# A second FFN with six seven-product blocks in place of five, and a last norm whose weight is multiplied in with the factor

## The chip, the cores and the metric

One core of a Trainium2 chip runs the whole layer. The metric is the device time of one execution in microseconds. The kernel before takes 2642.25 us (median of three runs, 2641.42 to 2644.68).

The engines appear under these names: PE is TensorE's matrix unit (PEld its weight loads), DVE is VectorE, ACT is ScalarE, POOL is GpSimd, SP is SyncE, which here only issues DMAs. Each engine runs its own queue in order.

## What is computed

The layer is a diffusion backbone block: a half-step SwiGLU FFN, a mixer (attention heads beside mLSTM heads), a second half-step SwiGLU FFN, and a final RMSNorm. The change lies in the second FFN and the final norm, which work on the 256 latent tokens alone. With `D` = 2048 and `D_FF` = 5632:

```python
def rms_norm(x, g):
    y = xf * lax.rsqrt(jnp.mean(xf * xf, axis=-1, keepdims=True) + RMS_EPS)
    return (y * g.astype(jnp.float32)).astype(x.dtype)

def adaln(x, g, mod, i):
    return rms_norm(x, g) * (1 + mod[:, i + 1, None, :]) + mod[:, i, None, :]

def half_step_ffn(x, mod, i, g, w_up, w_down):
    h = adaln(x, g, mod, i)
    a, b = jnp.split(h @ w_up, 2, axis=-1)
    return x + 0.5 * mod[:, i + 2, None, :] * ((jax.nn.silu(a) * b) @ w_down)
...
        xl = half_step_ffn(xl, mod_l, 6, g_norm[l, 2], w_ffn2_up[l], w_ffn2_down[l])
...
    return rms_norm(xl, g_final)
```

Everything is float32.

## The kernel before

**Products.** A float32 product is made of three matmuls in a faster format (`mm3`, L143 on): each operand is split into a high part and a low remainder, and high x high, high x low and low x high are added up in PSUM. Activations are split once. Each weight tile of 128x2048 is loaded from memory into `raw` (three buffers) and split by `split` in two halves of 128x1024: ScalarE writes `hi` (L123), VectorE writes `lo = raw - hi` (L124). `hi` and `lo` have four buffers each, so at most four half tiles are ready ahead of PE.

**Blocks.** The 5632 columns of the FFN are 11 blocks of 512 (`FB` = 4 tiles of 128), numbered 0 to 10; `LAST` is 10. Block 0 is made before the loop. For each block there is an up projection (both halves, `a` and `b`) and a down projection. `down(n)` has four units, one for each column block `cb` of the output: it loads one tile of `w_dn`, makes 12 matmuls for each of the two groups of 128 tokens, and adds the result to `acc2` in SBUF.

**Two kinds of up projection.** `up(n)` is the plain one, eight units: 2 halves x 4 weight tiles, 24 matmuls each, 192 in all. `quad(n)` makes the same block with seven products for eight: the normed activations are seen as 2x2 quarters (128 tokens x 1024 inputs), the weights as 2x2 quarters (1024 inputs x half `a` or `b`), and seven products of sums of quarters replace eight of plain quarters. The sums of activations (`n1`, `s4`, `s2`, `s3`) are made once by `token_forms`. Each product is two steps (`q` = 0 and 1, one weight tile of 128x2048 each) of 12 matmuls, so a quad has 14 steps and 168 matmuls, collected in two PSUM banks `X` and `Y`.

**Sums of weights in a quad.** The products need the weight quarters B11; B11+B12; B11+B12+B22; and all four, in this order, in two SBUF tiles `chain_[q]`; and B22 and then B12+B22 in two tiles `ra[q]`. `chain_[q]` is loaded plainly through SP, and then each further quarter is added by an accumulating DMA which POOL issues (`accum`, L696), as soon as the tile has been split for the product before. `ra[q]` is loaded with B22 through SP (`loaded`) and receives B12 by an accumulating DMA. `again` loads the first quarter of the next quad into `chain_[q]` after the last product's split. The list `order` in `quad` names for every product its activations, its weight tile, its PSUM bank, what is to follow the split (`then`) and what is done with the bank (`use`).

**Order.** `units()` yields the up and down units of the blocks made plainly and of all down projections; after each unit `u` the loop at the end of the function takes steps of the quads, until `n_side` reaches `(u + 1) * PACE2`. The results of a block are turned by PE (`turned`, four transposes for a block and a group of 128 tokens) into the layout that the down projection reads (`hids`, two buffers); `turned` waits until block n - 2 has been summed up, and `done` notes which results have been turned. A scheduler then orders the instructions of each engine by priority, where nothing pins them; `tc.keep_in_program_order` pins one.

**Beside it.** `beside["load"]` is an iterator which `load_split` advances once for every plain unit: it carries the 32 items of the modulation rows 8 (`mod_late`, a VectorE multiply-and-sum of 128x1024 for each, L203), and at their end `mod_rows_out` (L355): a transpose, a copy by VectorE, and a DMA of the row to memory. `before_final` then loads that row into all partitions as `late["g8"]`, and the norm's weight as `late["gf"]`, into the places of `chain_`. The last down blocks need `g8` (`half_gated`, L980).

**The end.** Block 9's down projection adds the gate and, by an accumulating DMA, the residual to `acc2`. `last2` makes block 10's down projection and the final norm, for each group of 128 tokens: for each column block, gate (L982), add, square and sum on ScalarE (`sumsq`), multiply by `gf` (L2183). After the fourth sum: a reduction on VectorE, `rsqrt_mean` on POOL (two instructions: a multiply-add, and a power of -1/2), then the factor times the column blocks, shared between ScalarE and VectorE, and the output's DMAs.

Of the kernel before, what the change touches and what calls it, by code (L numbers as in the profile page):

```python
# [9 lines left out]
F32 = mybir.dt.float32  # L10
# [9 lines left out]
P = 128  # L20
# [13 lines left out]
PACE = (4, 2), (12, 13), (19, 19), (26, 28), (33, 37), (37, 44), (42, 51), (48, 54), (52, 61), (55, 70), (58, 76), (59, 85), (63, 96)  # L34
PACE += (70, 102), (72, 109), (75, 118), (76, 130), (77, 144), (80, 152), (83, 163), (85, 166), (86, 174), (96, 181)

PACE2 = 70 / 73

BLOCKS2 = tuple((k, k + 4) for k in range(0, 16, 4))

# [14 lines left out]
def tile_layer(ctx: ExitStack, tc: tile.TileContext, I: dict, out: bass.AP):  # L55
# [641 lines left out]
    with pool(name="f1u", bufs=1) as f1u:  # L697
# [16 lines left out]
        def part(n, ab, c):  # L714
            return I["w_up1b"][n - 1, ab, c]
# [1119 lines left out]
    with f2x:  # L1835
# [54 lines left out]


        LAST = NF // FB - 1
        QUADS = range(1, LAST, 2)

        def part(n, ab, c):
            return I["w_up2b"][n - 1, ab, c]
# [85 lines left out]
        def quad(n):  # L1982
# [38 lines left out]
            def chained(ab, c):  # L2021
                return lambda q: accum(chain_[q], part(n, ab, c + q))

            def again(q):
                if n + 2 in QUADS:
                    nc.sync.dma_start(chain_[q], part(n + 2, 0, q))

            def loaded(q):
                ra[q] = ra_tile()
# [3 lines left out]
            def plain(q):  # L2033
# [5 lines left out]
            order = (  # L2039
                (a11, held, "X", True, chained(1, 0), p1),  # L2040
                (a12, plain, "Y", True, None, c11),
                (n1, held, "Y", True, chained(1, 2), kept),
                (s4, loaded, "Y", False, lambda q: accum(ra[q], part(n, 1, q)), p35),
                (s2, held, "X", False, chained(0, 2), c12),
                (s3, lambda q: ra[q], "X", False, None, c22),
                (a22, held, "Y", True, again, c21),
# [49 lines left out]
        def down(n):  # L2096

            assert (n, 1) in done or not n
            for cb in range(NCB):
                wt = load_split(I["w_dn2"][n, cb])  # L2100
                for t in range(2):
                    c = slice(cb * CB, (cb + 1) * CB)
                    b = block(n, wt, t)
                    a = acc2[:, t, c]
                    if n == 0:
                        nc.scalar.activation(a, b, AF.Copy)
                    else:
                        nc.vector.tensor_tensor(a, a, b, op=ALU.add)
                    if n == LAST - 1:
                        half_gated(a, a, late["g8"][:, c])  # L2110
                        accum(a, x2d[t * P : (t + 1) * P, c])
                if cb == NCB - 1:
                    summed.add(n)
                yield

        def units():
            yield from up(2)
            yield from down(0)
            for n in (4, 6, 8):
                yield from up(n)  # L2120
                yield from down(n - 3)
                yield from down(n - 2)
            yield from down(7)
            yield from up(10)
            yield from down(8)

        def before_final():
            drain(beside["load"])
# [6 lines left out]
        def quads():  # L2135
            for n in QUADS:
                yield from quad(n)

        forms = token_forms()
        side, n_side, n_quads = quads(), 0, 14 * len(QUADS)  # L2140
        for u, _ in enumerate(units()):
            steps(forms)
            turned()
            while n_side < n_quads and n_side < (u + 1) * PACE2:
                next(side)
                n_side += 1
                turned()
# [7 lines left out]
        def last2():  # L2155

            parts = []
            for cb in range(NCB):
                if cb >= 2:
                    parts.append(load_split(I["w_dn2"][LAST, cb]))  # L2160
                    continue
                raw = raw_tile()
                nc.sync.dma_start(raw, I["w_dn2"][LAST, cb])
                hi = f3.tile([P, 2048], F32R, tag=f"f{2 * cb}", name=f"hi{cb}")
                lo = f3.tile([P, 2048], F32R, tag=f"f{2 * cb + 1}", name=f"lo{cb}")
                nc.scalar.activation(hi, raw, AF.Copy)
                nc.vector.tensor_tensor(lo, raw, hi.bitcast(F32), op=ALU.subtract)
                parts.append(lambda w, hi=hi, lo=lo: (hi[:, w], lo[:, w]))
            for t in range(2):
                ss = sm.tile([P, 4], F32, tag="ss4", name="ss4", bufs=4)  # L2170
                for cb in range(NCB):
                    c = slice(cb * CB, (cb + 1) * CB)
                    b = block(LAST, parts[cb], t)
                    a = acc2[:, t, c]
                    y = sab_tile()
                    half_gated(y, b, late["g8"][:, c])
                    nc.vector.tensor_tensor(a, a, y, op=ALU.add)
                    sumsq(ss[:, cb : cb + 1], a)
                    if cb == NCB - 1:
                        s1 = sm.tile([P, 1], F32, tag="s1", name="s1")  # L2180
                        nc.vector.tensor_reduce(s1, ss, axis=AX.X, op=ALU.add)
                        r = rsqrt_mean(s1, D)
                    nc.vector.tensor_tensor(a, a, late["gf"][:, c], op=ALU.mult)  # L2183
                for cb in range(NCB):
                    c = slice(cb * CB, (cb + 1) * CB)
                    a = acc2[:, t, c]
                    if t == 0 or cb % 2:
                        nc.scalar.activation(a, a, AF.Copy, scale=r)
                    else:
                        nc.vector.tensor_scalar(a, a, r, None, op0=ALU.mult)  # L2190
                    nc.sync.dma_start(out[t * P : (t + 1) * P, c], a)

        last2()

# [95 lines left out]
```

## Time and profile before

| what | us |
|---|---|
| median of three runs | 2642.25 |
| the profiled execution | 2649.92 |
| its span (first to last instruction) | 2648.2 |
| PE busy in the span | 2598.3 (98%) |
| VectorE busy in the span | 2123.5 (80%) |
| ScalarE busy in the span | 1365.9 (52%) |
| mean granted TensorE clock | 0.994 |

How to read the rows of the profile below. A row of the view by stretch gives the stretch in us, its length, the busy time and number of instructions of PE, PEld, DVE, ACT and POOL, the mean granted clock, the mean busy share of the 16 DMA engines and GB/s. A row of waits gives who waited for whom, the total in us, how often, and the longest. A row of the timeline gives the start in us, the duration, engine, line, operation and shapes; in brackets stands the idle time before it and what ended it. A row of the chain that ended last gives start, duration and instruction. A row of a group of instructions gives their number, busy time, mean ns of one, and the idle time of the engine just before them with what ended it. A row of DMA issues gives the number, the size of one and the median us from issue to landing; "DMA to landing" gives the shortest, median and longest of one line.

### The profile page before, as it was taken

To read this page: it belongs to the slowest core of one execution; us is meant where nothing else is said; L and a number is where in the kernel's file an instruction comes from. 1 tells how busy PE (TensorE), PEld (TensorE's weight loads), DVE (VectorE), ACT (ScalarE), POOL (GpSimd) and SP (SyncE) were. 2 spreads that over 40 slices of the span, in tenths; PEclk is the share of its full clock that TensorE was granted. 3 is DMA by queue.
4 is the path that set the end of the run, shared out by engine and by line. 5 is a ranking of instruction groups with operands and counts; after the bars stand their busy time and mean duration, and the time that the engine had idled before them with its cause. 6 is when DMAs were issued, how large, how long until landed. Compare 5 with 4: busy or idle time off the path is not lost. (4 is left out here: it accounts for less than half of the span.)

```text
span 2648.2 us, 33739 instructions
## 1 busy us (share of the span) xinstructions
PE 2598.3 (98%) x12718; PEld 2154.5 (81%) x12718; DVE 2123.5 (80%) x2854; ACT 1365.9 (52%) x1741; POOL 221.9 (8%) x271
## 2 busy tenths in 40 slices
PE   7999999999999999999999999999999999999998
PEld 4688887888788878888879989877898888888886
DVE  7697878878888788888887878788788777777867
ACT  4354444554444555444455438455476655555554
POOL 1000001000001000000111000111000000000001
PEclk8999999999999999999999999999999999999999
DMA  9879999999999989889986855666679998989975
GB/s 371 331 222 266 266 279 262 256 276 281 256 273 260 284 232 244 212 218 226 226 249 248 310 199 195 243 210 215 217 253 288 303 294 283 286 286 279 272 232 169
DMA packets 127219, 679.97 MB, mean 257 GB/s; under 512 B 14152, under 2 KB 16712, under 8 KB 65232
## 3 DMA queue, kind: packets, MB, share of 16 engines
q1 hardware_dynamic: 99696, 500.59, 50.9%
q0 software_dynamic: 27360, 177.22, 34.2%
q8 instruction: 100, 1.64, 0.2%
q14 instruction: 63, 0.52, 0.1%
HBM read 659.87 MB, written 17.89 MB: 256 GB/s over the span
## 5 line engine op out<-in xcount | busy, mean ns | idle before, releaser
L123 ACT ACTIVATE hi<-raw 128x1024 fp32r<-128x1024 f32 (+2 forms) x538 | 558.1, 1042 | 600.5 <-PE mm L147 454.0
L124 DVE TENSOR_TENSOR lo<-raw,hi 128x1024 fp32r<-128x1024 f32 (+1 forms) x524 | 630.6, 1210 | 254.0 <-ACT hi L123 229.6
L123 ACT ACTIVATE hi<-chain 128x1024 fp32r<-128x1024 f32 x320 | 337.8, 1059 | 259.0 <-PE mm L147 128.5
L124 DVE TENSOR_TENSOR lo<-chain,hi 128x1024 fp32r<-128x1024 f32 x320 | 387.1, 1221 | 99.3 <-ACT hi L123 96.8
L145 PE MATMUL mm<-hi,hhi 128*128 128x512 f32 (+3 forms) x1024 | 394.1, 386 | 7.0 <-DVE c L799 7.0
L147 PE MATMUL mm<-hi,hlo 128*128 128x512 f32 (+3 forms) x1024 | 388.4, 379 | 0.0
L146 PE MATMUL mm<-lo,hhi 128*128 128x512 f32 (+3 forms) x1024 | 388.0, 379 | 0.2
L203 DVE SCALAR_TENSOR_TENSOR junk<-sraw,cBh 128x1024 fp8e5<-128x1024 f32 x192 | 234.2, 1220 | 23.7 <-DMA sraw<-in_w_mt 21.4
L145 PEld LDWEIGHTS mm<-hi,hhi 128*128 128x128 f32 x1024 | 192.8, 189 | 39.6 <-ACT hi L123 4.5
L147 PEld LDWEIGHTS mm<-hi,hlo 128*128 128x128 f32 x1024 | 193.1, 189 | 33.9
L146 PEld LDWEIGHTS mm<-lo,hhi 128*128 128x128 f32 x1024 | 193.3, 189 | 31.8 <-DVE lo L124 0.6
L147 PE MATMUL mm<-hi,hid2l 128*128 128x512 f32 x352 | 137.4, 390 | 0.0
L145 PE MATMUL mm<-hi,hid2h 128*128 128x512 f32 x352 | 137.2, 390 | 0.0
L146 PE MATMUL mm<-lo,hid2h 128*128 128x512 f32 x352 | 137.1, 390 | 0.0
L145 PE MATMUL mm<-hi,h2hi 128*128 128x512 f32 x320 | 124.7, 391 | 0.6 <-DVE sab L1874 0.6
L146 PE MATMUL mm<-lo,h2hi 128*128 128x512 f32 x320 | 124.8, 390 | 0.1
L147 PE MATMUL mm<-hi,h2lo 128*128 128x512 f32 x320 | 124.6, 389 | 0.0
L696 POOL DMA_DIRECT2D chain<-in_w_up1b x60 | 53.1, 884 | 743.5 <-DVE lo L124 582.8
L145 PE MATMUL mm<-hhi,hi 128*128 128x512 f32 (+1 forms) x288 | 101.2, 351 | 0.0
L147 PE MATMUL mm<-hhi,lo 128*128 128x512 f32 (+1 forms) x288 | 99.0, 344 | 0.0
L146 PE MATMUL mm<-hlo,hi 128*128 128x512 f32 (+1 forms) x288 | 98.7, 343 | 0.0
L203 DVE SCALAR_TENSOR_TENSOR sr<-sr,cBl 128x1024 f32<-128x1024 f32 x65 | 78.9, 1225 | 8.7 <-DMA sr<-in_w_mt 8.6
(492 smaller groups left out, 5477.1 us busy)
## 6 DMA issues: line engine op xcount, KB each, us to landing
raw<-in_w_dn SPq DMA_DIRECT2D x70, 1024.0 KB, 7.4
sraw<-in_w_mt SPq DMA_DIRECT2D x128, 512.0 KB, 7.7
chain<-in_w_up1b POOLq DMA_DIRECT2D x60, 1024.0 KB, 10.7
raw<-in_w_up2b SPq DMA_DIRECT2D x50, 1024.0 KB, 7.0
raw<-in_w_up1b SPq DMA_DIRECT2D x40, 1024.0 KB, 8.2
mraw<-in_w_m SPq DMA_DIRECT2D x32, 1024.0 KB, 7.2
sr<-in_w_mt SPq DMA_DIRECT2D x62, 512.0 KB, 5.3
chain<-in_w_dn POOLq DMA_DIRECT2D x30, 1024.0 KB, 8.4
```

Of the source, the lines that this page charges most:

```text
L123: scalar[0].activation(hi, src, AF.Copy)
L124: vector[0].tensor_tensor(lo, src, hi.bitcast(F32), op=ALU.subtract)
L145: tensor[0].matmul(out_ap, sh, mh, start=first, stop=False, skip_group_check=skip)
L146: tensor[0].matmul(out_ap, sh, ml, start=False, stop=False, skip_group_check=skip)
L147: tensor[0].matmul(out_ap, sl, mh, start=False, stop=last, skip_group_check=skip)
L203: ins = nc.vector.scalar_tensor_tensor(junk() if junk else raw, raw, 1.0, cB[s], op0=ALU.mult, op1=ALU.mult, accum_out=mT[:, i, s, kt, h : ...
L696: accum = lambda dst, src: nc.gpsimd.dma_start(dst, src, accum_op=ALU.add)
```

## The change

- The blocks made with seven products are 1, 3, 5, 6, 7 and 9 in place of 1, 3, 5, 7 and 9; block 6 was plain before. `PACE2` becomes 84 / 68: 84 quad steps beside 68 units (70 beside 76 before).
- The third quarter, B22, is no longer added to `chain_` by an accumulating DMA after product `n1`. `ra` holds it already, so VectorE adds `ra[q]` to `chain_[q]` after the split for product `s4` (`summed_weights`); the accumulating DMA of B12 into `ra[q]` follows that add.
- The order of units is written as a list, and `ready` holds a quad step back until results of the quad before have been turned.
- In `last2` the multiplication by `gf` is delayed by one column block (`gain`); that of the last column block is joined with the factor in one VectorE instruction. The multiply-add ahead of the power moves from POOL to VectorE. Column blocks 0 and 1 are scaled by ScalarE, 2 and 3 by VectorE, and the outputs are issued in the order 0, 3, 1, 2.

```diff
-PACE2 = 70 / 73
+PACE2 = 84 / 68
...
-        QUADS = range(1, LAST, 2)
+        QUADS = (1, 3, 5, 6, 7, 9)
...
+            def summed_weights(q):
+
+                ins = add(chain_[q], chain_[q], ra[q])
+                tc.keep_in_program_order(ins)
+                accum(ra[q], part(n, 1, q))
+
             def again(q):
-                if n + 2 in QUADS:
-                    nc.sync.dma_start(chain_[q], part(n + 2, 0, q))
+                if n != QUADS[-1]:
+                    nc.sync.dma_start(chain_[q], part(QUADS[QUADS.index(n) + 1], 0, q))
...
-                (n1, held, "Y", True, chained(1, 2), kept),
-                (s4, loaded, "Y", False, lambda q: accum(ra[q], part(n, 1, q)), p35),
+                (n1, held, "Y", True, None, kept),
+                (s4, loaded, "Y", False, summed_weights, p35),
...
         def units():
-            yield from up(2)
-            yield from down(0)
-            for n in (4, 6, 8):
+            for n, downs in ((2, (0, 1)), (4, (2, 3, 4)), (8, (5, 6)), (10, (7, 8))):
                 yield from up(n)
-                yield from down(n - 3)
-                yield from down(n - 2)
-            yield from down(7)
-            yield from up(10)
-            yield from down(8)
+                for d in downs:
+                    yield from down(d)
...
+        def ready(i):
+
+            n, step = i // 14, i % 14
+            if step == 11:
+                return (QUADS[n], 0) in done
+            return not n or step not in (1, 7) or (QUADS[n - 1], step // 7) in done
+
...
-            while n_side < n_quads and n_side < (u + 1) * PACE2:
+            while n_side < n_quads and n_side < (u + 1) * PACE2 and ready(n_side):
...
+            def gain(t, cb):
+                a = acc2[:, t, cb * CB : (cb + 1) * CB]
+                tc.keep_in_program_order(nc.vector.tensor_tensor(a, a, late["gf"][:, cb * CB : (cb + 1) * CB], op=ALU.mult))
+
...
-                    if cb == NCB - 1:
-                        s1 = sm.tile([P, 1], F32, tag="s1", name="s1")
-                        nc.vector.tensor_reduce(s1, ss, axis=AX.X, op=ALU.add)
-                        r = rsqrt_mean(s1, D)
-                    nc.vector.tensor_tensor(a, a, late["gf"][:, c], op=ALU.mult)
-                for cb in range(NCB):
+                    if cb:
+                        gain(t, cb - 1)
+                s1 = sm.tile([P, 1], F32, tag="s1", name="s1")
+                nc.vector.tensor_reduce(s1, ss, axis=AX.X, op=ALU.add)
+                r = sm.tile([P, 16], F32, tag="rstd", name="rstd", bufs=4)[:, :1]
+                tc.keep_in_program_order(nc.vector.tensor_scalar(r, s1, 1.0 / D, EPS, op0=ALU.mult, op1=ALU.add))
+                tc.keep_in_program_order(nc.gpsimd.tensor_tensor(r, r, mhalf[:, :1], op=ALU.pow))
+                for cb in (3, 0, 2, 1):
                     c = slice(cb * CB, (cb + 1) * CB)
                     a = acc2[:, t, c]
-                    if t == 0 or cb % 2:
+                    if cb == 3:
+
+                        tc.keep_in_program_order(nc.vector.scalar_tensor_tensor(a, a, r, late["gf"][:, c], op0=ALU.mult, op1=ALU.mult))
+                    elif cb == 2:
+                        tc.keep_in_program_order(nc.vector.tensor_scalar(a, a, r, None, op0=ALU.mult))
+                    else:
                         nc.scalar.activation(a, a, AF.Copy, scale=r)
-                    else:
-                        nc.vector.tensor_scalar(a, a, r, None, op0=ALU.mult)
-                    nc.sync.dma_start(out[t * P : (t + 1) * P, c], a)
+                for cb in (0, 3, 1, 2):
+                    c = slice(cb * CB, (cb + 1) * CB)
+                    nc.sync.dma_start(out[t * P : (t + 1) * P, c], acc2[:, t, c])
```

## The prediction

> **What bounds the kernel now.** I read the page's busy shares first, then busy time by stretch over the second FFN, then TensorE's waits there, then the matmuls in order of time.
>
> ```profile
> span 2648.2 us, 33739 instructions
> PE 2598.3 (98%) x12718; PEld 2154.5 (81%) x12718; DVE 2123.5 (80%) x2854; ACT 1365.9 (52%) x1741; POOL 221.9 (8%) x271
> ...
> core 0: us, PE busy (x) PEld busy (x) DVE busy (x) ACT busy (x) POOL busy (x), PEclk, DMA share, GB/s
> 1985.00:2570.00 585.00, 584.92 (x2613) 483.24 (x2612) 449.66 (x472) 334.63 (x350) 34.93 (x40) 1.00 0.92 281
> 2300.00:2350.00 50.00, 50.00 (x230) 41.30 (x229) 42.38 (x49) 28.05 (x30) 1.73 (x2) 1.00 0.84 280
> 2630.00:2648.20 18.20, 7.45 (x33) 5.82 (x31) 9.11 (x16) 6.68 (x14) 1.85 (x4) 0.78 0.33 115
> ...
> PE mm L145 <- DVE sab L1874: 0.6, 1, 0.6
> ```
>
> In the 585 us that the edit rearranges PE is busy for 584.92, and its only recorded wait after 1980 us is 0.6 us at the start. VectorE is busy 77% and the DMA engines 92%, yet neither makes PE wait. A busy PE need not be a dense one, so I measure the step from one matmul to the next:
>
> ```profile
> 1979.52 0.50 PE L145 MATMUL mm<-hi,h2hi 128*128 128x512 f32 x1 [0.58 <-DVE sab L1874]
> ...
> 1985.09 0.39 PE L145 MATMUL X<-hi,h2hi 128*128 128x512 f32 x1
> ...
> 1987.81 0.39 PE L145 MATMUL mm<-hi,h2hi 128*128 128x512 f32 x1
> ...
> 2637.06 0.39 PE L147 MATMUL mm<-hi,hid2l 128*128 128x512 f32 x1
> ...
> 2574.45 0.44 PE tr L1963 x4
> ```
>
> Twelve matmuls lie between the second and the third row: 2.72 / 12 = 0.2267 us each (0.39 is a latency, and they overlap). By the code, 5 plain up projections of 192 matmuls, 5 quads of 168 and 11 down blocks of 96 follow the first row: 2,856 matmuls, 647.4 us. Twenty groups of four transposes at 0.44 add 8.8. That is 656.2 of the 657.8 us from the first row to the end of the last matmul: PE is the bound, within 0.3%. So time leaves only by fewer matmuls or a shorter end, and comes in as new waits of PE.
>
> **The matmuls removed.** Five plain blocks and five quads become four and six: 768 + 1,008 + 1,056 = 2,832, 24 fewer. 24 x 0.2267 = 5.4 us. Transposes stay at twenty groups. The built program's order confirms both and shows no more than two quad steps beside one unit, so the new readiness test bunches nothing further.
>
> **VectorE's new work.** The rows for it:
>
> ```profile
> L124 DVE TENSOR_TENSOR lo<-raw,hi 128x1024 fp32r<-128x1024 f32 x164 | 199.6, 1223 | 122.0 <-ACT hi L123 121.9
> L123 ACT ACTIVATE hi<-raw 128x1024 fp32r<-128x1024 f32 x164 | 173.0, 1060 | 187.5 <-PE mm L147 163.0 <-DMA raw<-in_w_up2b 11.7 <-DMA raw<-in_w_dn 3.5
> L2108 DVE TENSOR_TENSOR acc<-acc,mm 128x512 f32<-128x512 f32 x56 | 38.1, 681 | 1.9 <-PE mm L147 1.9
> ...
> 2603.22 2.28 DVE L2167 TENSOR_TENSOR lo<-raw,hi 128x2048 fp32r<-128x2048 f32 x1
> ```
>
> No 128x2048 add of two weight tiles is in this trace; the nearest row is L2167, the same shape with two SBUF inputs: 2.28 us. Two per quad, six quads: 27.4. A quad splits 14 tiles, a plain block 8, so one exchange adds 12 half splits of 1.22 = 14.6, and some four small adds of 0.68 = 2.7. VectorE goes from 449.7 of 585 to 494 of 580 us, 85%. The window 2300 to 2350 already stands at 42.38 of 50, also 85%, with PE at 50.00. What hides the work is reserve: VectorE's idle time before splits ends with ScalarE's high parts, whose own waits end with PE giving a buffer back. With four buffers of half tiles, of which a quad uses one in 1.36 us and a plain or down unit one in 2.72, the reserve is at most 8.2 us of matmuls.
>
> The densest spot is an s4 step beside a down unit (in quads 5, 7 and 9). PE has 36 matmuls, 8.2 us; VectorE has four half splits, 4.9, the add, 2.3, two accumulations, 1.4, and every other time a modulation item of about 1.3: 8.5 to 9.8. Two such steps in a row draw 1 to 3 us from the reserve. If the cover were gone, each add would cost up to 2.28, together 27.4; if it holds, nothing. Below nothing is excluded, since PE lost nothing to splits there. I take 0.4, near the hidden end, by that window.
>
> At the start the reserve is empty already:
>
> ```profile
> 2010.58 1.21 DVE ra L1912
> 2011.79 1.15 DVE lo L124
> ...
> 2012.98 0.50 PE mm L146
> ```
>
> VectorE still makes the token forms there, and PE lost 0.27 us (0.50 for a step of 0.23). Units 0 to 3 now hold five quad steps in place of four: 35.4 us of matmuls against 39 of VectorE, where before it was 32.6 against 36.5. The gap stays near 4 us, but the first two adds follow at once. Between 0 and 2.3 us; by the order, the split of unit 4 comes some 0.25 late, so I take 0.3.
>
> **DMA and queues.**
>
> ```profile
> chain<-in_w_up2b POOLq DMA_DIRECT2D x30, 1024.0 KB, 10.9
> chain<-in_w_up2b SPq DMA_DIRECT2D x8, 1024.0 KB, 6.1
> DMA to landing us min/median/max: 7.1/8.1/9.2
> ```
>
> Accumulating loads go from 40 to 36, tile loads from 70 to 68: less traffic, worth nothing, as PE waits for none. The accumulation into `ra` now waits for the add behind its split, and POOL holds only the later accumulations behind it. Its 10.9 us run until product s3, four quad steps and at least three units later: 4 x 2.72 + 3 x 5.44 = 27 us. At three quad boundaries (3 to 5, 5 to 6, 7 to 9) the next quad's first tile is asked of SP when the old one is split, some 11.3 us (48 matmuls, four transposes) before its matmuls; 6.1 fits, and 9.2 (the slowest of the first two such loads, third row) may miss by 1 to 2 us. I take nothing.
>
> **The end of the units.** Before, the quads ended three units early; now the last product is followed at once by block 9. Two chains matter:
>
> ```profile
> 2571.73 0.69 DVE L1984 TENSOR_TENSOR ca<-Y,ca 128x512 f32<-128x512 f32 x1
> ...
> 2542.53 0.27 DVE L360 COPY gr<-tr 16x128 f32<-16x128 f32 x1
> 2542.83 0.33 SPq L361 DMA_DIRECT2D mod<-gr  x1
> ...
> 2557.25 0.33 SPq L2132 DMA_DIRECT2D g<-mod  x1
> ...
> g<-mod SPq DMA_DIRECT2D x1, 1024.0 KB, 4.6
> mod<-gr SPq DMA_DIRECT2D x1, 8.0 KB, 3.3
> DMA to landing us min/median/max: 2.4/3.9/5.8
> raw<-in_w_dn SPq DMA_DIRECT2D x3, 1024.0 KB, 7.0
> ```
>
> First, the turn: from L1984 to the transposes took 2574.45 - 2571.73 = 2.7 us; the new order puts 12 matmuls there, 2.7 us, of which the first overlap the product's drain: 0.3 lost. Second, the modulation items advance once per unit. With 68 units in place of 76 their end meets the end of the units, and gate row `g8`, asked for at 2557.25 before, is now made during block 9. From its transpose to its landing: copy with its wait in line 0.9, SP 0.3, 3.3, 4.6, about 9.1 us. Then VectorE has eight instructions of 0.6 and a split of 1.1 ahead of the split that PE needs next: 15.1. PE has 70 matmuls, 15.9, until then. SP's later weight loads stand behind the gate row's. The spare 0.8 is lost if the row's first DMA takes 5.8 (the longest of that line), or if the last block's first tile takes 7.0 us: 0 to 2.5, I take 0.7.
>
> **The last norm.**
>
> ```profile
> 2637.69 0.69 DVE L2183 TENSOR_TENSOR acc<-acc,gf 128x512 f32<-128x512 f32 x1 [0.85 <-ACT junk L158]
> 2638.30 0.68 DVE L982 SCALAR_TENSOR_TENSOR sab<-mm,g 128x512 f32<-128x512 f32 x1
> ...
> 2640.56 0.16 DVE L2181 TENSOR_REDUCE s<-ss 128x1 f32<-128x4 f32 x1 [0.85 <-ACT junk L158]
> ...
> 2640.80 0.56 POOL L152 TENSOR_SCALAR rstd<-s 128x1 f32<-128x1 f32 x1 [9.98 <-DVE s L2181]
> 2641.45 0.55 POOL L153 TENSOR_TENSOR rstd<-rstd,mhalf 128x1 f32<-128x1 f32 x1
> 2642.03 1.33 ACT L2188 ACTIVATE acc<-acc,rstd 128x512 f32<-128x512 f32 x2 [1.50 <-POOL rstd L153]
> ```
>
> The last matmul ends near 2637.45, but L982 waits until 2638.30 behind the weight's multiplication (L2183), which waits for the squares of its own column block. One block later in line it waits for nothing: 0.8 us. POOL's first step, 0.65 with its handover, becomes a 128x1 VectorE instruction; the nearest row is the 0.16 of L2181: 0.4 saved. The multiplication that joins the factor (0.68) takes the place of one of ScalarE's 0.66, and the first output leaves some 0.2 later. Together 1.1 saved, between 0.4 and 1.3.
>
> The sum: -5.4 - 1.1 + 0.4 + 0.3 + 0.3 + 0.7 = -4.8 on the execution's span of 2648.2; it took 2649.92 with what lies around it, and the runs' median is 2642.25. The difference carries over: 2637.5 us.
>
> **The rivals.**
> A, the forecast: 2637.5, between 2636.5 and 2639.5 as the four small terms fall.
> B, every cover holds: -6.5, 2635.7. For it: PE is dense before beside windows of 85% VectorE. Against: the end's spare is under 1 us.
> C, the end's chain is late: with a landing of 5.8 for the row and 7.0 for the tile the two add up to some 4 us, and each microsecond more is paid in full: 2640 to 2645. For it: SP's loads stand behind the wait. Against: the DMA engines are idler at the end (0.33 in the last window). The granted clock speaks here too: it reads 0.78 over the last window, most of which PE is idle.
> [...]
> D, VectorE becomes the bound at the adds. Its place is the s4 steps; it decides once the reserve is under 2.28 us there. Half of the 27.4 paid gives 13.7 - 6.5 = +7.2, 2649.4; it is slower by over 0.2% once 11.8 of the 27.4 (five adds of twelve) are paid. For it: queue order, two adds within three steps. Against: 122.0 us of idle time before splits now, and 85% without a wait.
>
> **How the numbers follow.** 0.2% is 5.3 us, about what a measurement of this kernel tells from no change. A has 0.45, B 0.30, C 0.15, D 0.10. Faster than 2637.0 are B and under a quarter of A: 0.40. Within are the rest of A and C: 0.50. Slower is D: 0.10. A's own range is 2636.5 to 2639.5. The range that I give, 2635.0 to 2646.5, takes in B with 0.7 us for the scatter of runs, and C; D and the far ends stay outside.
>
> **What would show it.** Right: 2,832 matmuls 0.2267 apart; VectorE near 85% with PE still at 50.00 in each 50 us from 2050; the factor's scaling some 3.3 us after the last matmul's end (4.6 before). Wrong: PE waits for `lo` right after the adds (D), PE idle between the gate row's transpose and the last block (C), or waits of ScalarE for `chain` loads at the quad boundaries.

## The result, and the profile after

The changed kernel took 2652.64 us (median of 11 runs, 2648.17 to 2654.92), the kernel before, on the same chip, 2644.68 us (2641.42 to 2647.30). The ratio is 1.0028, with a 95% interval of 1.002 to 1.0036: slower by 7.4 us by that ratio (5.3 to 9.5), where 4.8 us less was forecast.

The work ahead of the second FFN is the same in both kernels, yet its end moves by some 10 us from one profiled execution to the next. I mark it by the first matmul behind block 0 of the second FFN (block 0's own up projection, the same in both, lies before it; the texts below call this matmul the second FFN's first). It came between 1970.5 and 1980.1 us in the fourteen traces of this study. So I compare the **stretch** from that matmul to the end of the span: 2648.2 - 1979.52 = 668.7 us before, 2648.7 - 1975.13 = 673.6 us after, 4.9 us more. Two kernels below (e2 beside the one before, e3 beside the changed one) come within 0.1 us of the stretch of the kernel they were made from, so I read it to some tenths of a microsecond. What lies between 4.9 and the 7.4 of the timed runs is not explained; a kernel below with the same stretch (673.6) measured +4.5 us.

The first lines of the changed kernel's page, for comparison with those shown of before:

```profile
span 2648.7 us, 33736 instructions
PE 2594.7 (98%) x12694; PEld 2149.5 (81%) x12694; DVE 2163.9 (82%) x2884; ACT 1379.2 (52%) x1755; POOL 217.1 (8%) x265
```

The 24 matmuls are gone (12,718 to 12,694). Now busy time by window, of the changed kernel: the 585 us that the edit rearranges, and the stage from the matmul named above to the last.

```profile
core 0: us, PE busy (x) PEld busy (x) DVE busy (x) ACT busy (x) POOL busy (x), PEclk, DMA share, GB/s
1985.00:2570.00 585.00, 579.37 (x2572) 474.89 (x2571) 482.21 (x490) 342.29 (x358) 30.37 (x35) 1.00 0.86 268
1975.13:2637.64 662.51, 656.12 (x2913) 537.74 (x2913) 550.00 (x575) 382.98 (x407) 39.00 (x45) 1.00 0.83 260
```

The same view of the kernel before, from the same matmul to its last:

```profile
1979.52:2637.06 657.54, 657.46 (x2936) 543.37 (x2937) 511.63 (x547) 369.68 (x394) 43.02 (x50) 1.00 0.89 272
```

PE was idle for 0.1 us before; now it idles for 6.4 of 662.5 us. VectorE is busy 82% of the middle (77% before) and the DMA engines 0.86 (0.92 before): neither is used up. A waiting matmul costs more than its recorded wait: the one at 2000.60 below has 0.46 us recorded, but starts 0.86 us after the one before it, and the next follows after 0.34. So I measure the steps between matmuls and count as lost what exceeds 0.2267 us by over 0.05 (and 0.44 for four transposes that stand between): 2.2 us before, 11.9 us after, 9.8 us more. With still smaller excesses that is where the 5.4 us of removed matmuls went, with 4.9 on top. The places are in TensorE's waits of the changed kernel (in total, times, longest):

```profile
PE tr L1963 <- DVE ca L1985: 2.5, 2, 1.5
PE Y L146 <- DVE lo L124: 2.0, 4, 0.6
PE mm L146 <- DVE lo L124: 1.4, 4, 0.5
PE Y L145 <- ACT cy L1998: 0.2, 1, 0.2
```

**The start** (4.1 us lost in the first 50 us, 0.5 before). Instructions of the changed kernel in order of time, by engine (start, duration, in brackets the idle time before and what ended it):

```profile
1986.80 0.33 SPq L2041 DMA_DIRECT2D raw<-in_w_up2b  x1
...
1998.22 2.01 ACT L123 ACTIVATE hi<-raw 128x1024 fp32r<-128x1024 f32 x2 [5.32 <-DMA raw<-in_w_up2b]
...
1999.32 1.23 DVE L124 TENSOR_TENSOR lo<-raw,hi 128x1024 fp32r<-128x1024 f32 x1 [3.46 <-ACT hi L123]
...
1999.74 0.39 PE L145 MATMUL Y<-hi,h2hi 128*128 128x512 f32 x1
2000.60 0.50 PE L146 MATMUL Y<-lo,h2hi 128*128 128x512 f32 x1 [0.46 <-DVE lo L124]
```

The second weight tile for `a12` lands 11.3 us after its issue; ScalarE waits 5.32 us for it, VectorE 3.46 behind ScalarE, and PE reaches the low part before it exists. With two steps after the first unit, this tile is wanted one unit earlier than before. It is also asked for earlier (11.7 us after the stretch begins in place of 17.5), but now two accumulating loads are issued 3.4 us apart just ahead of it (8.0 before). The same tile in the kernel before was issued at 1997.05:

```profile
2005.91 2.01 ACT L123 ACTIVATE hi<-raw 128x1024 fp32r<-128x1024 f32 x2 [3.18 <-DMA raw<-in_w_up2b]
```

There ScalarE waited 3.18 us, for a load of at most 8.9, and PE did not wait. In the changed kernel VectorE, which still makes the token forms, stays late until 2015. 0.5 of the 4.1 us is another thing, a wait at a PSUM bank at 2023, which e5 below explains.

**Two block boundaries** (1.2 and 1.7 us lost, from quad 3 to 5 and 7 to 9). The first of them, changed kernel, in order of time by engine:

```profile
2170.74 4.54 SPq L2032 DMA_DIRECT2D chain<-in_w_up2b  x2
...
2177.74 2.01 ACT L123 ACTIVATE hi<-chain 128x1024 fp32r<-128x1024 f32 x2 [1.42 <-DMA chain<-in_w_up2b]
...
2178.83 1.23 DVE L124 TENSOR_TENSOR lo<-chain,hi 128x1024 fp32r<-128x1024 f32 x1 [1.26 <-ACT hi L123]
2179.98 0.68 DVE L1984 TENSOR_TENSOR ca<-Y,ca 128x512 f32<-128x512 f32 x1
...
2181.71 0.69 DVE L1985 TENSOR_TENSOR ca<-ca,cy 128x512 f32<-128x512 f32 x1
...
2182.54 0.63 PE L1963 MATMUL tr<-ident,ca 128*128 128x128 f32 x4 [0.98 <-DVE ca L1985]
```

Here both steps of the last product follow one unit, so the next quad's first tile is asked for late; it takes 6.9 us. ScalarE and VectorE split it at the head of their queues, and the finished block's sum (L1984), its `silu` and its product (L1985) stand behind that split. The block is turned late, though nothing it needs was late.

**The end.** The gate row and the last weight tiles, changed kernel, by engine:

```profile
2598.11 0.32 SPq L361 DMA_DIRECT2D mod<-gr  x1
2600.72 0.33 SPq L2133 DMA_DIRECT2D g<-mod  x1
...
2621.99 2.01 ACT L123 ACTIVATE hi<-raw 128x1024 fp32r<-128x1024 f32 x2 [9.52 <-DMA raw<-in_w_dn]
...
2624.36 0.50 PE L146 MATMUL mm<-lo,hid2h 128*128 128x512 f32 x1 [0.50 <-DVE lo L124]
...
2639.17 0.68 DVE L982 SCALAR_TENSOR_TENSOR sab<-mm,g 128x512 f32<-128x512 f32 x1
...
2642.43 1.33 ACT L2207 ACTIVATE acc<-acc,rstd 128x512 f32<-128x512 f32 x2 [1.04 <-POOL rstd L2197]
```

The last matmul starts at 2637.64 and is done some 0.4 later, but VectorE comes to its result only at 2639.17, without a wait of its own: it has been behind since the last tiles. So the scaling starts 4.4 us after the last matmul's end, where 3.3 was forecast and 4.6 stood before. From the last matmul to the end are 11.06 us, 11.14 before. The tile that ScalarE waits for at 2621.99 took 8.5 us from issue to landing, and PE lost 0.8 us there.

Two more waits for VectorE's low parts, in down units, cost 0.5 us at 2241 and 0.9 at 2520. The second stands in e4 and e6 too, is gone in e8, and was not traced further. Ahead of the first VectorE works without a pause, and the second addition of quad 5 is part of it:

```profile
2237.45 2.28 DVE L1984 TENSOR_TENSOR chain<-chain,ra 128x2048 f32<-128x2048 f32 x1
2239.65 0.68 DVE L2114 TENSOR_TENSOR acc<-acc,mm 128x512 f32<-128x512 f32 x1
2240.25 2.36 DVE L124 TENSOR_TENSOR lo<-raw,hi 128x1024 fp32r<-128x1024 f32 x2
```

### The profile page after: what moved, and what is told of

Its sections match the earlier page's. It is cut to its first block, busy times and chain, and to the rows that moved or that the text cites. A ratio compares the mean times of both kernels' runs of the same rounds, so it can differ in the third digit from the quotient of the medians.

```text
span 2648.7 us, 33736 instructions
## 1 busy us (share of the span) xinstructions
PE 2594.7 (98%) x12694; PEld 2149.5 (81%) x12694; DVE 2163.9 (82%) x2884; ACT 1379.2 (52%) x1755; POOL 217.1 (8%) x265
## 5 line engine op out<-in xcount | busy, mean ns | idle before, releaser
L123 ACT ACTIVATE hi<-raw 128x1024 fp32r<-128x1024 f32 (+2 forms) x526 | 545.4, 1042 | 558.5 <-PE mm L147 398.7
L124 DVE TENSOR_TENSOR lo<-raw,hi 128x1024 fp32r<-128x1024 f32 (+1 forms) x512 | 615.3, 1211 | 208.3 <-ACT hi L123 182.4
L123 ACT ACTIVATE hi<-chain 128x1024 fp32r<-128x1024 f32 x336 | 354.5, 1059 | 278.3 <-PE mm L147 143.3
L124 DVE TENSOR_TENSOR lo<-chain,hi 128x1024 fp32r<-128x1024 f32 x336 | 406.9, 1222 | 108.9 <-ACT hi L123 106.9
L145 PE MATMUL mm<-hi,h2hi 128*128 128x512 f32 x256 | 99.9, 392 | 0.6 <-DVE sab L1874 0.6
L146 PE MATMUL mm<-lo,h2hi 128*128 128x512 f32 x256 | 100.1, 391 | 0.2 <-DVE lo L124 0.2
L147 PE MATMUL mm<-hi,h2lo 128*128 128x512 f32 x256 | 99.7, 390 | 0.0
## 6 DMA issues: line engine op xcount, KB each, us to landing
chain<-in_w_up1b POOLq DMA_DIRECT2D x60, 1024.0 KB, 10.6
```

Of the source, the lines that this page charges most:

```text
L123: scalar[0].activation(hi, src, AF.Copy)
L124: vector[0].tensor_tensor(lo, src, hi.bitcast(F32), op=ALU.subtract)
L145: tensor[0].matmul(out_ap, sh, mh, start=first, stop=False, skip_group_check=skip)
L146: tensor[0].matmul(out_ap, sh, ml, start=False, stop=False, skip_group_check=skip)
L147: tensor[0].matmul(out_ap, sl, mh, start=False, stop=last, skip_group_check=skip)
```

## The experiments

"Lost" is counted as above; "tail" runs from the last matmul's start to the end of the span. All from one trace each; the ratio is to the kernel before, on the same chip.

| kernel | stretch | lost, first 50 us | lost, later | tail | median, ratio (95%) |
|---|---|---|---|---|---|
| before | 668.7 | 0.5 | 1.7 | 11.1 | |
| after | 673.6 | 4.1 | 7.8 | 11.1 | 2652.64, 1.0028 (1.002 to 1.0036) |
| e1 last norm alone | 667.4 | 0.3 | 1.8 | 9.9 | 2643.57, 1.0 (0.9989 to 1.0011) |
| e2 VectorE's sums alone | 668.7 | 0.3 | 1.7 | 11.1 | 2644.52, 0.9996 (0.9987 to 1.0005) |
| e3 one step after unit 0 | 673.6 | 3.7 | 8.2 | 11.1 | 2648.86, 1.0017 (1.0006 to 1.0028) |
| e4 gate row early | 669.3 | 4.5 | 4.2 | 10.0 | 2644.98, 1.0002 (0.9991 to 1.0012) |
| e5 row early, pairs by hand | 667.7 | 0.2 | 6.6 | 10.0 | 2644.63, 0.9996 (0.9987 to 1.0005) |
| e6 as e4, sums by load | 675.3 | 6.4 | 8.5 | 10.0 | 2650.50, 1.002 (1.0011 to 1.0029) |
| e7 as e5, old last norm | 670.9 | 0.2 | 6.9 | 13.0 | 2645.81, 1.0005 (0.9996 to 1.0014) |
| e8 row early, banks apart | 662.4 | 0.2 | 2.0 | 10.0 | 2639.05, 0.9977 (0.9967 to 0.9986) |
| e9 the same, other pairs | 662.2 | 0.2 | 1.9 | 10.0 | 2639.10, 0.9977 (0.9966 to 0.9988) |
| e10 as e8, row late | 663.6 | 0.2 | 2.3 | 10.6 | 2640.51, 0.9984 (0.9975 to 0.9993) |
| e11 as e8, sums by load | 663.4 | 0.3 | 2.9 | 10.0 | 2640.72, 0.9981 (0.9972 to 0.999) |
| e12 as e8, old last norm | 664.6 | 0.2 | 2.2 | 11.9 | 2642.18, 0.9989 (0.998 to 0.9998) |

### One part of the change alone, in the kernel before

**e1**: the last norm of the change in the kernel before.

```diff
-                    nc.vector.tensor_tensor(a, a, late["gf"][:, c], op=ALU.mult)
+                    if cb:
+                        gain(t, cb - 1)
...
-                        r = rsqrt_mean(s1, D)
+                tc.keep_in_program_order(nc.vector.tensor_scalar(r, s1, 1.0 / D, EPS, op0=ALU.mult, op1=ALU.add))
+                tc.keep_in_program_order(nc.gpsimd.tensor_tensor(r, r, mhalf[:, :1], op=ALU.pow))
```

> The kernel before with the last norm's edit alone. All theories: the factor's scaling starts 3.3 to 3.6 us after the last matmul's end in place of 4.6, and the time falls by 0.4 to 1.3 us (ratio 0.9995 to 0.9998). If VectorE's wait for POOL's power in the first token group holds up the second group's gating, the scaling starts no earlier than 4.2 us after the last matmul and the time stays (ratio 1.0000).

The stretch is 1.3 us shorter, all of it in the tail. The trace of this kernel, VectorE's last gate and ScalarE's scaling (the last matmul started at 2628.04):

```profile
2628.46 0.69 DVE L982 SCALAR_TENSOR_TENSOR sab<-mm,g 128x512 f32<-128x512 f32 x1 [0.70 <-PE mm L147]
...
2631.74 1.33 ACT L2199 ACTIVATE acc<-acc,rstd 128x512 f32<-128x512 f32 x2 [1.04 <-POOL rstd L2189]
```

VectorE waits for PE here (0.70), and the scaling comes 3.3 us after the last matmul's end: the forecast step, at the upper end of its bounds. In the changed kernel VectorE was the late one, and of this gain 0.1 was left.

**e2**: the sums by VectorE in the five quads of before, at their old pace.

```diff
-                (n1, held, "Y", True, chained(1, 2), kept),
-                (s4, loaded, "Y", False, lambda q: accum(ra[q], part(n, 1, q)), p35),
+                (n1, held, "Y", True, None, kept),
+                (s4, loaded, "Y", False, summed_weights, p35),
```

> The kernel before with VectorE's weight sum in place of the accumulating load in its five quads, all else unchanged. Theory V (VectorE's adds are what costs): ten adds, half of them paid, +5 to +14 us. Theory S (loads land late where the faster pace crowds accumulating and plain loads together) and theory R (the gate row's chain at the end): no change, within 1.5 us of before, with PE's gaps in the stage at 3 us or less.

The stretch is the same to 0.1 us. Ten additions of 2.3 us on VectorE cost nothing where PE's order stays: rival D falls at the old pace.

### The changed kernel with one thing put elsewhere

**e3**: one step of the quads after the first unit in place of two.

```diff
-            while n_side < n_quads and n_side < (u + 1) * PACE2 and ready(n_side):
+            while n_side < n_quads and n_side < (u + 1) * PACE2 - (u == 0) and ready(n_side):
```

> The changed kernel with one quad step beside the first unit in place of two, so that the first two accumulating loads are not issued 3.4 us apart; all else as changed. Theory S: PE's gaps before 2025 us fall from 3.4 to under 1 us, the time from +7.4 to about +4.5 us. Theories V and R: the start is not the cause, the time stays at +7 and PE's gaps there stay above 2.5 us.

A miss: 0.4 us less at the start, 0.4 more later, the stretch the same. The pair had only moved to the next unit, and `a12` was wanted as early as in the changed kernel. The first two accumulating loads are 8.0 us apart here, and `a12`'s second tile lands in 7.6 us without a wait of PE. But ScalarE waits 5.57 us for the next plain tile, and PE stands there in its place. So the spacing of the loads alone does not cure the start.

**e4**: the modulation items at a quicker pace, so that row `g8` is made before the last block.

```diff
-        beside["load"] = mod_late(f8cm.__enter__(), 8, 9, ((32, 62),))
+        beside["load"] = mod_late(f8cm.__enter__(), 8, 9, ((32, 50),))
```

> The changed kernel with the modulation items spread over 50 in place of 62 advances, so that the gate row is made some ten units earlier; all else as changed. Theory R: no wait of VectorE or ScalarE for the row or for loads behind it after the last transpose, the scaling starts near 3.4 us after the last matmul, and the time falls by 1.5 to 3 us, to about +5. Theories V and S: at most 0.5 us less.

The stretch falls by 4.3 us: 1.1 in the tail, 0.8 in the last products and 2.9 in the middle, where both boundary waits are gone; the start's loss stays (0.4 more). At the second boundary the load lands in time. At the first, ScalarE waits for it as long as in the changed kernel (1.49 us here, 1.42 there), but VectorE's queue reads otherwise, and so do the transposes behind it:

```profile
2178.24 0.69 DVE L1984 TENSOR_TENSOR ca<-Y,ca 128x512 f32<-128x512 f32 x1
2178.84 1.22 DVE L124 TENSOR_TENSOR lo<-chain,hi 128x1024 fp32r<-128x1024 f32 x1
2179.97 0.69 DVE L1985 TENSOR_TENSOR ca<-ca,cy 128x512 f32<-128x512 f32 x1
...
2180.81 0.63 PE L1963 MATMUL tr<-ident,ca 128*128 128x128 f32 x4
```

The sum stands ahead of the split now, with a modulation item before both, and the turn isn't late (no wait of PE at 2180.81): the late load alone costs nothing here, the place in the queue decides. The row is a part of the loss, and not the whole.

### The pairs of steps set by hand

The changed kernel has two steps after 16 of its 68 units, wherever `(u + 1) * 84 / 68` passes two whole numbers within a unit. From here on the units with two steps are a list; the row is early as in e4 unless said otherwise.

**e5**: no pair in the first seven units, then evenly. The text below has a step of `n1` or `s3` in each pair; the list made it so in ten of the sixteen, `n1` with `s4` and `s3`'s two steps five times each. Five more are `a11`'s second step with `a12`'s first, and one is `s4` with `s2`.

```diff
-PACE2 = 84 / 68
+TWO = (7, 9, 13, 16, 20, 24, 27, 31, 35, 38, 42, 46, 49, 53, 57, 60)
...
-            while n_side < n_quads and n_side < (u + 1) * PACE2 and ready(n_side):
+            while n_side < n_quads and n_side < u + 1 + sum(x <= u for x in TWO) and ready(n_side):
```

> Changed kernel with the gate row's items early (as in the run before it) and the 16 units that are followed by two steps of the quads set by hand: none in the first seven units (while VectorE also makes the token forms and the first weights land 11 us after their issue), the others evenly, each with a step of n1 or s3 in it, which load nothing. Theory P (crowding at the start is what is left: two steps in one unit while VectorE and the DMA ring are both full): the gaps of TensorE in the first 50 us fall from 4.5 us to under 1, the stretch from the second FFN's first matmul to the end of the span goes from 669.3 us to 664.5 to 666, and the time to 2638 to 2641.5 us, 3 to 6 below the kernel before. Theory V (VectorE at over 83% has no room for six blocks: what is removed at the start comes back later): the gaps move to the middle, the stretch stays at 668 to 670 and the time at 2643 to 2646.

The start's loss is gone, 4.5 to 0.2 us. But 2.4 us more are lost later than in e4 (6.6 against 4.2): neither theory's numbers. Its waits of PE, and the instructions of one place:

```profile
PE mm L146 <- DVE lo L124: 0.7, 2, 0.4
PE Y L145 <- ACT cy L1998: 0.7, 4, 0.2
PE mm L145 <- ACT hid2h L1966: 0.2, 1, 0.2
```

```profile
2325.21 0.60 ACT L1998 ACTIVATE cy<-Y 128x512 f32<-128x512 f32 x1 [0.30 <-PE Y L147]
...
2325.01 0.69 PE L145 MATMUL mm<-hi,h2hi 128*128 128x512 f32 x2
2325.86 0.50 PE L145 MATMUL Y<-hi,s4f 128*128 128x512 f32 x1 [0.17 <-ACT cy L1998]
```

My list put `n1`'s second step and `s4`'s first after one unit in five of six quads (16, 27, 38, 49 and 60). Both use bank `Y`, and ScalarE has to copy `n1`'s result out of it before `s4` adds to it. With two matmuls between them, and no unit, PE waits: 0.17 us recorded and 0.5 lost at four places, 0.4 at the fifth. In the changed kernel the same pair stands twice, at 2023 and 2329 us, and costs 0.5 each time.

**e8** and **e9**: no pair of `n1` with `s4` or of `s2` with `s3`; in e8 the pairs are `a12`'s two steps, `s4` with `s2`, and `s3` with `a22`, in e9 `n1`'s two, `s2`'s two, and `s3` with `a22` (its first pair is `s4` with `s2`, as in e8). The last product ends one unit earlier.

```diff
-TWO = (7, 9, 13, 16, 20, 24, 27, 31, 35, 38, 42, 46, 49, 53, 57, 60)
+TWO = (7, 10, 14, 18, 21, 25, 29, 32, 36, 40, 43, 47, 51, 54, 58, 62, 65)
```

(and in e9 7, 10, 16, 19, 21, 27, 30, 32, 38, 41, 43, 49, 52, 54, 60, 63, 65)

> As the kernel whose doubled steps were set by hand (gate row early), with the doubled steps moved so that n1's second step and s4's first are never in one unit (they share a bank that ACT copies between them: the waits of s4's matmul for that copy were 0.4 us each), likewise s2's and s3's, and the last block's seventh product one unit earlier. The doubled pairs are now a12's two steps, s4's second with s2's first, s3's second with a22's first. Theory B (short waits for a bank's copy, made by doubling, ate the rest): the gaps in the middle fall from 5.1 us to under 2.5, the stretch from 667.7 us to 664 to 665.5, the time to 2639 to 2642. Theory V (VectorE is late by turns wherever two steps meet, at 83% of the stage): as many gaps return behind other steps, the stretch is 667 to 669 and the time 2643 to 2646.

> As the kernel before it in this group, with n1's two steps (which load nothing), s2's two and s3's second with a22's first as the pairs: less even in time, but never two steps of a12, whose weights come through the ring of raw tiles, nor a step of s4 with its two additions on VectorE, in one unit. Theory B: stretch 664 to 665.5 us as well, within 0.7 us of the other. If the DMA ring is what doubling a12 strains, this one is shorter by 1 us or more; if evenness counts most, it is longer by 1 us or more. Theory V: 667 to 669 us for both.

Both run at 0.9977 of the kernel before, -6.1 us (-3.7 to -8.7 for e8). The window of e8 from the first matmul of the stretch to its last:

```profile
1974.55:2626.86 652.31, 652.29 (x2913) 538.65 (x2913) 552.30 (x577) 381.95 (x409) 39.02 (x45) 1.00 0.85 264
```

PE is busy for 652.29 of 652.31 us, with VectorE at 85% of it. The stage is 657.54 - 652.31 = 5.2 us shorter than before, of 5.4 forecast, and the tail 1.1. So six blocks have room on every engine. That e8 and e9 agree within 0.2 us says that neither two steps of `a12` nor evenness decides. e5 lost 4.6 us more than e8; its trace has 2.4 at the bank, 1.8 at waits for VectorE's low parts, and 0.6 at the turn after the last product, which came one unit later there. These were not tried one by one.

### The parts, in either order of steps

**e6** (as e4) and **e11** (as e8): each quad's sum by accumulating loads again.

```diff
-                (n1, held, "Y", True, None, kept),
-                (s4, loaded, "Y", False, summed_weights, p35),
+                (n1, held, "Y", True, chained(1, 2), kept),
+                (s4, loaded, "Y", False, lambda q: accum(ra[q], part(n, 1, q)), p35),
```

> Changed kernel with the gate row's items early, and the weight sum of each quad by an accumulating load again in place of VectorE's two additions (14 MB more through the queue of POOL, 12 x 1.2 us less on VectorE). Theory V (VectorE's additions are what the six quads lack room for): the gaps in the first 50 us fall by 2 us or more and the stretch to the end from 669.3 to 665 to 667, the time to 2639.5 to 2642.5. Theory P (two steps in a unit crowd the loads at the start): the start's gaps stay at 4 us or grow, the stretch is 669 to 672 and the time 2644 to 2648.

> The kernel with n1 and s4 apart and the row early, but each quad's weight sum by accumulating loads again, as in the kernel before, in place of VectorE's two additions. If the additions only shift work from the loads to VectorE at no cost either way, the stretch stays within 0.7 us of 662.4. If six blocks at this pace need the loads that the additions save (at the first pace the accumulating loads made the stretch 6 us longer), it is 664.5 to 668 us and the time 2 to 6 us longer. Theory V would have it shorter, under 661.5.

Twelve loads of 1 MB come in and twelve additions of 2.28 us go (not the 14 MB and 1.2 us of the first text). In the formula's order the stretch is 6.0 us longer (669.3 to 675.3). But 1.9 of it, at the start, cannot be the loads': PE's waits there begin at 1996, and the first extra load is issued at 2011. 3.8 more lie at 2029 to 2036 us, where a tile took 13.9 us to land and the granted clock fell from 1.00 to 0.50 (the last section shows the place). In e8's order the stretch is 1.0 us longer (662.4 to 663.4), above the 0.7 of "no cost either way"; 0.9 of it is one place, where PE waits for a plain tile that took 9.3 us to land:

```profile
2309.56 2.01 ACT L123 ACTIVATE hi<-raw 128x1024 fp32r<-128x1024 f32 x2 [2.86 <-DMA raw<-in_w_up2b]
...
2311.93 0.50 PE L146 MATMUL mm<-lo,h2hi 128*128 128x512 f32 x1 [0.65 <-DVE lo L124]
...
1978.75:2632.12 653.37, 652.70 (x2913) 538.53 (x2913) 527.74 (x565) 381.64 (x409) 49.39 (x57) 1.00 0.93 283
```

Theory V falls at the new pace too: taking the additions away made both kernels longer. The DMA engines stand at 0.93 in e11 and PE at 652.70 of 653.37; VectorE has 25 us less to do than in e8. The additions move work from the loads to VectorE; by these traces they save about 1 us once the steps are well placed, and some 4 in the formula's order.

**e7** (as e5) and **e12** (as e8): the last norm of the kernel before.

```diff
-                    if cb:
-                        gain(t, cb - 1)
+                    nc.vector.tensor_tensor(a, a, late["gf"][:, c], op=ALU.mult)
```

> As the first kernel of this group (row early, doubled steps set by hand), but with the last norm of the kernel before. If the last norm's part is worth what it was alone (1.3 us of the stretch, in which nothing of VectorE was late), the stretch is 1.0 to 1.6 us longer than the first kernel's and the time 1 to 2 us more. If VectorE's lateness over the last products eats it, as in the changed kernel, the two agree within 0.4 us.

> The kernel with n1 and s4 apart and the row early, with the last norm of the kernel before. If the last norm's part is worth what it was alone (1.3 us), the stretch is 663.4 to 664.0 us. If it is worth what it was beside the first hand-set order (3.2 us), 665 to 666.

The new norm is worth 3.2 us beside e5's order and 2.2 beside e8's, between the two guesses for e12, against 1.3 alone in e1. Both of e7's guesses missed (1.0 to 1.6, or under 0.4). The traces show where it comes from: the old norm's multiplications by `gf` wait in VectorE's queue for ScalarE's squares (2.33 us once in e7, behind ScalarE's scaling of the first token group), and the last scaling starts 6.3 us after the last matmul's end in e7 and 5.3 in e12, against 4.6 in the kernel before. Why they wait longer beside six blocks was not followed up.

**e10** (as e8): the row late, as in the changed kernel.

> The kernel with n1 and s4 apart (662.4 us from the second FFN's first matmul to the end of its span), but the gate row's items at the changed kernel's late place. Theory R (that place alone makes VectorE and the last loads late at the end, and crowds the block boundaries): gaps of 1 to 3 us return, most of them in the last 60 us, the tail goes from 10.0 back to about 11, and the stretch is 664.5 to 666.5 us, the time 2 to 4 us over the early row's. Theory O (the late row hurt only beside badly placed doubled steps): within 0.5 us of 662.4, and the time within 1.5 us of the early row's.

+1.3 us (0.6 of it in the tail), short of theory R's 2 and beyond theory O's 0.5. From the changed kernel to e10 only the pairs move, and the stretch falls by 673.6 - 663.6 = 10.0 us; from the changed kernel to e4 only the row, and it falls by 4.3; both together give 11.2. So most of what the row costs it costs beside badly placed pairs.

## Why the prediction was wrong

The mechanism that the change is built on was right, and so were most terms of the sum. **The matmuls**: 5.4 forecast, 5.2 in e8. **VectorE's additions**: 0.4 forecast within 0 and 27.4; each took 2.28 us, as estimated, and 0.5 us was lost behind one of them in the changed kernel (2241 us); e2 adds ten at no cost, and taking them out makes e6 and e11 longer. So the size that rival D needs is refuted by three kernels, though its sign showed once. **The turn after the last product**: 0.3 forecast, 0.6 lost. **The last norm**: 1.1 forecast within 0.4 and 1.3; 1.3 in e1, but 0.1 in the changed kernel, because VectorE reached the last block 1.1 us after PE had finished it: the step took for granted that PE comes last there.

**The step that failed** is the sentence that the order "shows no more than two quad steps beside one unit, so the new readiness test bunches nothing further". I took two steps per unit as harmless and priced the rest by averages over units. Moving only the pairs (e10) gives back 10.0 us. Three things hide under that sentence.

**The start**, 0.3 taken, 0 to 2.3 in bounds, 3.7 measured (4.1 against 0.5; 0.5 of it at a bank). The working compared VectorE's 39 us with PE's 35.4 and left the loads out, on the ground that PE waits for none before. ScalarE stood idle for 5.32 us (3.18 before) until the tile for `a12`, wanted a unit earlier, had landed, and that ran the chain ScalarE, VectorE, PE dry. The changed kernel, e4 and e6 have the same order up to there; the tile took 11.3, 11.7 and 13.7 us to land, and the start lost 4.1, 4.5 and 6.4. That points to the loads. But in e3 that tile lands in 7.6 us and the next one is waited for, so the early pair is the cause that the runs show (e5 and e8 have none there, and lose 0.2), and how much of it is the loads' is open. (In the row at 2012.98 the prediction took 0.50, a duration, for the step; the step is 0.46.)

**The boundaries**: "I take nothing", with 1 to 2 us for a landing of 9.2. Measured were 1.2 and 1.7 us, at landings of 6.9 and 7.4. I compared the landing with the time until the next quad's own matmuls; the place where it was paid is VectorE's queue, in which the old block's sum stood behind the waiting split. e4 has the same wait of ScalarE, another order, and no loss.

**The banks**: not in the prediction at all. A product that adds to a bank still being copied cost about 0.5 us where only two matmuls lay between. It happened twice in the changed kernel and five times in e5.

**The gate row**, 0.7 taken within 0 and 2.5. The row landed no later than forecast (4.6, and 2.6 for its first DMA in place of 3.3), but the last tile took 8.5 us, where C counted with 7.0. In e10 the late place costs 1.3, inside the bounds; in the changed kernel 4.3, with the boundaries. The forecast of rival C (2640 to 2645) had the place, but not that the items reach back into the boundaries. The granted clock, of which C speaks, played no part in the changed kernel: it reads 1.00 in every 5 us from the first matmul of the stretch to the last.

The chances went wrong with it: slower had 0.10, all of it on VectorE's additions, and none on the order of steps. That no wait is recorded in a dense stretch was read as reserve everywhere; it was the property of one order.

## What to carry to other kernels

When two streams of work are interleaved on a bound engine, a new ratio between them is an edit to the order, and has to be checked step by step: which tile is wanted earlier, which queue has a wait at its head with other blocks' work behind it, and which accumulator is still being read. Averages by stage do not tell a dense order from another: VectorE and the DMA engines stand at 85% and 0.85 in e8, and at 83% and 0.83 in the changed kernel, whose stage is 10 us longer. Here a list of 17 positions and an earlier row turned 7.4 us slower into 6.1 us faster.

## What the runs showed of the hardware

TensorE's granted clock fell from 1.00 to 0.50 at one place in e6, behind short waits. Matmuls in order of time, and the granted clock (the first figure after POOL's busy time) of two windows there:

```profile
2029.31 0.39 PE L147 MATMUL mm<-hi,h2lo 128*128 128x512 f32 x1
2030.60 0.49 PE L145 MATMUL Y<-hi,s4f 128*128 128x512 f32 x1 [0.91 <-ACT hi L123]
2031.86 0.53 PE L146 MATMUL Y<-lo,s4f 128*128 128x512 f32 x1 [0.77 <-DVE lo L124]
2032.20 0.62 PE L147 MATMUL Y<-hi,s4f 128*128 128x512 f32 x1
2032.62 0.63 PE L145 MATMUL Y<-hi,s4f 128*128 128x512 f32 x1
```

```profile
2033.00:2034.00 1.00, 1.00 (x4) 0.77 (x3) 1.00 (x2) 0.39 (x1) 0.65 (x1) 0.50 0.95 262
2036.00:2037.00 1.00, 1.00 (x6) 0.78 (x5) 0.45 (x1) 0.72 (x2) 0.00 (x0) 1.00 0.79 258
```

Two steps of 1.29 and 1.26 us, each with one matmul and a recorded wait (0.91 and 0.77), and from 2032.2 to 2035.6 matmuls come 0.425 us apart in place of 0.227, with the clock at 0.50 in the first window and back at 1.00 in the second: about 1.6 us for eight of them, on top of the waits. Waits of this length were not followed by it each time. Earlier in the same trace a matmul at 1995.58 was followed by these:

```profile
1997.72 0.50 PE L145 MATMUL Y<-hi,h2hi 128*128 128x512 f32 x1 [1.76 <-ACT hi L123]
1998.98 0.51 PE L146 MATMUL Y<-lo,h2hi 128*128 128x512 f32 x1 [0.76 <-DVE lo L124]
1999.33 0.39 PE L147 MATMUL Y<-hi,h2lo 128*128 128x512 f32 x1
1999.55 0.39 PE L145 MATMUL Y<-hi,h2hi 128*128 128x512 f32 x1
```

Steps of 2.14 and 1.26 us, with recorded waits of 1.76 and 0.76, and the matmuls after them are 0.22 us apart; the clock reads 1.00 from 1995 to 2005. What sets the two places apart was not shown.
